# Two solve steps a tick in the second delta-rule unit, other PSUM banks and block order for the output projection, and one product less per norm

## The chip, the cores and the metric

The kernel runs on one NeuronCore of one Trainium2 chip. The metric is the device time of one execution in microseconds; the time of a kernel is the median of its runs. The engines are TensorE (PE, with its weight loads as PEld), VectorE (DVE), ScalarE (ACT), GpSimd (POOL) and SyncE (SP, which issues nearly all DMAs here). Each has its own queue of instructions and works it off in order; they wait for one another by semaphores.

## The reference

One decoder layer over 256 tokens of width 2048, float32. Batch and depth are 1.

```
h = rms_norm(x, ln1)
qkv_a, beta_a, decay_a, z_a, qkv_b, gate_a, gate_b = split(h @ w_in)
y_a = gated_deltanet(qkv_a, beta_a, decay_a, z_a) @ w_branch_a      # 8 heads of 128, chunked delta rule
y_b = moba_attention(rope(q_b), rope(k_b), v_b) @ w_branch_b        # one block of 256: causal attention
x = x + (sigmoid(gate_a) * y_a + sigmoid(gate_b) * y_b) @ w_out
u_gate, u_val = split(causal_dwconv(rms_norm(x, ln2) @ w_up))       # 2 x 5632 channels, width 3
x = x + (silu(u_gate) * u_val) @ w_down
return rms_norm(x, final_norm)
```

The delta rule needs, per head and chunk of tokens, the inverse of a unit lower triangular matrix (`triangular_solve`), and its output is normed per head before it is gated with silu(z_a).

## The kernel before

**Products.** Every weight is split in two parts, high and low (`wh`, `wl`), and so is every activation; three products of parts stand for one float32 product. `load_w` fetches a weight block of 128 x 2048 (SP's queue, four `wraw` buffers), ACT casts it to `wh` in two halves and DVE subtracts to get `wl` (`split`, `low`). There are two `wh`/`wl` buffers, so a block's cast waits until PE has done with the block before the last. `chunk` makes an output of 2 x 128 channels from two blocks, `by_token` (gates, values, z, branches) one of 2 x 128 tokens x 512 channels in two accumulators, from blocks with 4 x 128 input channels each. A gate chunk has 96 products of 512 columns, 24 for each weight block.

**Stages in order.** Input norm and the delta rule's projections, values and z; the attention's projections (`ps_moba`); eight gate chunks (`ps_gate`, the loop at L756); the branch projections (`ps_br`, L800); the output projection (`ps_wo`, L819); 44 chunks of the up-projection (`ps_up`); the down projection (`pd`), the last norm and the output.

**Work in the background.** Heads are worked on in two units of four. `gdn_pair`, `gdn_unit`, `moba` and `merged` are generators in the list `bg`. `main_mm` counts the main products and calls `tick` after each EVERY = 1700 units (8 gate products): every generator in `bg` is advanced by one `yield`. So the generators' instructions are written in between the main products; a scheduler then sets the final order on each engine, within the dependences. `tc.issue_after(lows[-1].ins)` holds an instruction behind the last weight subtraction written so far.

**The unit's path.** `gdn_unit` solves the triangular blocks in 31 steps (L561; two DVE instructions each, on `X` and `tm`), with a `yield` after every second step in unit 0 and after every step in unit 1 (L566). Then X goes to DRAM and comes back as `TL` (POOL's queue, L568 and L570); after 12 ticks DVE transposes it in 32 x 32 blocks (L574). Two levels of products `py` and `pu` follow, then `u0`, `r1`, `u1`, the outputs `po`, POOL's square `so`, the head norm on DVE and ACT (L637 to L645), four ticks, the transposes `pot` and ACT's evictions into `ya`. Unit 1's tail waits for "gates", which is set right ahead of the gate chunks. At c == 4 the loop of L762 advances the generators until unit 1 is at its end; the gates' evictions for that chunk (`gts`, L769) are written behind it. After the eight chunks ACT casts `ya` and `yb` to `yca` and `ycb`, and POOL subtracts for their low parts (L781, L782).

**PSUM.** Up to the branches, pool `ps_mm` has three accumulators of one bank, `ps_sd` five. `psum_pools(3, 2)` then makes three of two banks (`wide`) and two of one. A new accumulator waits until what lay in its banks has been evicted (`reuse_waits="tile"`). For the first output chunk the steps at L821 run both blocks over input channels 0 to 11 and then over 12 to 15 (in units of 128), since `mc`, its input, gets channels 12 to 15 last: they come from `merged(3, i)`, which transposes on PE (`pt_m`) and splits on ACT and DVE (L797, L798).

**Norms.** `rstd` sums squares over channels with products against `ones` in float32 (`R1` at L300 from two tiles, `R2` at L844 from four).

Of the kernel before, what the change touches and what calls it, by code (L numbers as in the profile page):

```python
# [15 lines left out]
ALU = mybir.AluOpType  # L16
AX = mybir.AxisListType
PSUM = bass.MemoryType.PSUM
# [4 lines left out]
KD = D // P  # L23
# [50 lines left out]
def layer_kernel(ctx: ExitStack, tc: tile.TileContext, xT, pos, cst, ceye, vec, convw, ffw, bdv,  # L74
                 w_gdn, w_z, w_bd, w_moba, w_mv, w_gate, w_ba, w_bb, w_o, w_up, w_dn, fnorm, out):
    nc = tc.nc
    pe, act, dve, pool, sp = nc.tensor, nc.scalar, nc.vector, nc.gpsimd, nc.sync
# [8 lines left out]
    def mmg(ps, pairs, start=True, stop=True, **kw):  # L86
        n = len(pairs)
        for i, (a, b) in enumerate(pairs):
            pe.matmul(ps, a, b, start=(start and i == 0), stop=(stop and i == n - 1), **kw)  # L89
# [3 lines left out]
    def tick():  # L93
        for it in list(bg):
            if next(it, bg) is bg:
                bg.remove(it)
# [31 lines left out]
    def load_w(src, n=2048, into=None, piece=1024, raw=None):  # L128
        raw = raw or fetch(src, n)
        wh, wl = into or parts()  # L130
        for o in range(0, n, piece):
            lows.append(split(wh[:, o:o + piece], wl[:, o:o + piece], raw[:, o:o + piece]))
        return wh[:, :n], wl[:, :n]
# [10 lines left out]
    wide = [False]  # L144
    pst = [None, None, None]

    def psum_pools(mm, sd):
        if pst[2]:
            pst[2].close()
        pst[2] = ExitStack()  # L150
        pst[0] = pst[2].enter_context(tc.tile_pool(name="ps_mm", bufs=mm, space=PSUM, reuse_waits="tile"))
        pst[1] = pst[2].enter_context(tc.tile_pool(name="ps_sd", bufs=sd, space=PSUM, reuse_waits="tile"))

    psum_pools(3, 5)

    def mmt(name):
        return pst[0].tile([P, 2, 2, T] if wide[0] else [P, 2, T], F32, name=name, tag="mm")

    def sdt(name):
        return pst[1].tile([P, 512], F32, name=name, tag="sd")  # L160
# [12 lines left out]
    def chunk(blocks, x, kt, name, raws=(None, None), piece=1024, steps=((0, 0, None), (1, 0, None)), flush=None):  # L173
        ps = mmt("ps_" + name)
        ws = {}
        for n, (j, k0, k1) in enumerate(steps):
            while n == flush and bg:
                tick()
            if j not in ws:
                ws[j] = load_w(blocks[j], kt * P, raw=raws[j], piece=piece)  # L180
            block(ps[:, j], ws[j], x, kt, k0, k1)
        return ps
# [32 lines left out]
    def rstd(parts, tp, name):  # L215
        ps = sdt(name)[:, :T]
        mmg(ps, [(ones, t) for t in parts])
        r = tp.tile([P, T], F32, name=name)
        act.activation(r, ps, AF.Sqrt, bias=epst, scale=1.0 / D)
        dve.reciprocal(r, r)  # L220
        return r
# [9 lines left out]
    fk = front.enter_context(tc.tile_pool(name="fk", bufs=1))  # L231
# [51 lines left out]
    sq = []  # L283
# [5 lines left out]
        dve.tensor_tensor(sq[2], sq[2], sq[3], op=ALU.add)  # L289
    dve.tensor_tensor(sq[0], sq[0], sq[2], op=ALU.add)  # L290
    dve.tensor_tensor(sq[0][:, 0:2], sq[0][:, 0:2], sq[0][:, 2:4], op=ALU.add)


    wb2 = g.tile([P, KD, 48], F32R, name="wb2")
# [2 lines left out]
    low(wb2[:, :, 0:16], wb2[:, :, 32:48], wbd)  # L297
    s = sdt("ps_bd")[:48, :T]
    mmg(s, [(wb2[:, k, :], x_[:, k, :]) for k in range(KD) for x_ in (hh, hl)])
    R1 = rstd([sq[0][:, 0, :], sq[0][:, 1, :]], fk, "R1")  # L300
    R1b = both(R1)
    beta = fk.tile([16, T], F32, name="beta")
    sint = fk.tile([48, T], F32, name="sint")
# [81 lines left out]
    def decay():  # L385
        nz, ez, den, sv, s2, pv, spv, gt = (m.tile([16, T], F32, name=n, tag=t) for n, t in (
            ("nz", "qk0"), ("ez", "qk0"), ("den", "qk1"), ("sv", "qk1"), ("s2", "s_"), ("pv", "s_"),
            ("spv", "pT_"), ("gt", "pT_")))
        dve.tensor_tensor(z0, z0, R1[:16, :], op=ALU.mult)
        act.activation(beta, z0, AF.Sigmoid)  # L390
# [33 lines left out]
    def rms_columns():  # L424
        pt = sdt("pt_rms")
        for i in range(2):
            pe.transpose(pt[:, 16 * i:16 * i + 16], R1[:16, i * P:(i + 1) * P], ident[:16, :16])
        dve.tensor_copy(cols[:, 5:].rearrange("p a b -> p (a b)"), pt[:, :32])
# [110 lines left out]
    def gdn_unit(u):  # L539
# [21 lines left out]
        for r in range(30, -1, -1):  # L561
            tm = gu.tile([P, 8, 32], F32, name="tm", tag="Tm", bufs=1)
            n = 32 - r
            dve.tensor_tensor(tm[:, :, :n], X[:, :, r:], N[:, r:r + 1, r:].to_broadcast([P, 8, n]), op=ALU.mult)
            dve.tensor_reduce(X[:, :, r], tm[:, :, :n], axis=AX.X, op=ALU.add, negate=True)
            if r % (2 - u["n"]) == 0:  # L566
                yield
        pool.dma_start(bass.AP(tensor=dT.tensor, offset=dT.offset, ap=[[32 * P + 32, 32], [8 * P, 4], [P, 8], [1, 32]]), X)  # L568
        TL = gu.tile([P, 8, P], F32, name="TL", tag="u", bufs=1)
# [86 lines left out]
    def pair(w, i):  # L656
        return [w[2 * i], w[2 * i + 1]]
# [8 lines left out]
    for n in range(2):  # L666
        u = units[n]
# [3 lines left out]
        for pr in range(2):  # L671
# [3 lines left out]
            for a, t in enumerate((kq[:, 1], kq[:, 0], v)):  # L675
                if gr == 0 and a < 2:
                    ps = (ps_q0, ps_k0)[a]
                else:
                    ps = chunk(pair(w_gdn, 3 * gr + a), hc, KD, "gdn")
# [9 lines left out]
        if n == 0:  # L689
            bg.append(rotary())  # L690

            for c in range(2):
                ps = by_token(w_mv[4 * c:4 * c + 4], hc, KD, "ps_v")
# [49 lines left out]
    for gr in range(4):  # L743
        h0 = 2 * gr
        qk = []
        for a in range(2):
            ps = chunk(pair(w_moba, 2 * gr + a), hc, KD, "moba")
            t = m.tile([P, 2, T], F32, name=f"qk{a}")
# [7 lines left out]
    for c in range(8):  # L756
        ps = by_token(w_gate[4 * c:4 * c + 4], hc, KD, "ps_gate")
# [29 lines left out]
    mc = m.tile([P, KD * 2 * T + 128], F32R, name="mc")[:, SHIFT:SHIFT + KD * 2 * T].rearrange("p (k a t) -> p k a t", a=2, t=T)  # L787
# [12 lines left out]
    for c in range(4):  # L800
        ps = by_token(w_ba[2 * c:2 * c + 2], yc[0], H, "ps_br")
# [3 lines left out]
        ps = by_token(w_bb[2 * c:2 * c + 2], yc[1], H, "ps_br")  # L805
# [11 lines left out]
    sqa = b.tile([P, 2, T], F32, name="sqa", bufs=1)  # L817
    h2 = hp.tile([P, KD, 2, T], F32R, name="h2", tag="hc")
    for c in range(8):  # L819
        if c == 0:  # L820
            steps = ((0, 0, KD - 4), (1, 0, KD - 4), (0, KD - 4, KD), (1, KD - 4, KD))  # L821
            ps = chunk(pair(w_o, c), mc, KD, "wo", steps=steps, flush=2)
            y_st.close()
            bkeep = bk.enter_context(tc.tile_pool(name="bkeep", bufs=1, side="right", reuse_waits="tile"))
            x1 = bkeep.tile([P, KD, T], F32, name="x1")
            ffv = bkeep.tile([P, 88, 4], F32, name="ffv")
            sp.dma_start(ffv, ffw)
        else:
            ps = chunk(pair(w_o, c), mc, KD, "wo")
        if c % 2 == 0:  # L830
            s = slice(2 * c, 2 * c + 4)
            sp.dma_start(x1[:, s, :], xT[:, s, :])
        xc = x1[:, 2 * c:2 * c + 2, :]
        for a in (1, 0):
            dve.tensor_tensor(xc, xc, ps[:, :, a, :], op=ALU.add)
        scaled(xc, ln2v, 2 * c, h2[:, :, 0, :], h2[:, :, 1, :])
        if c == 0:
            act.activation(sqa, xc, AF.Square)
        else:
            sq = b.tile([P, 2, T], F32, name="sq2")  # L840
            act.activation(sq, xc, AF.Square)
            if c < 7:
                pool.tensor_tensor(sqa, sqa, sq, op=ALU.add)
    R2 = rstd([t[:, j, :] for t in (sqa, sq) for j in range(2)], bkeep, "R2")  # L844
    R2b = both(R2)
    bp.close()
    m_st.close()
# [4 lines left out]
    for c in range(NF):  # L852
        ps = chunk([w_up[c], w_up[NF + c]], h2, KD, "up")
        un = b.tile([P, 2, T], F32, name="unf")
        join(un, ps, R2b)
        t = b.tile([P, 2, T], F32, name="cvf")
# [15 lines left out]

    ps_d = ctx.enter_context(tc.tile_pool(name="ps_d", bufs=1, space=PSUM, reuse_waits="tile"))
    pd = [[ps_d.tile([P, 512], F32, name=f"pd{i}_{n}") for n in range(4)] for i in range(2)]
    order = [(1, 2), (1, 3), (0, 2), (0, 3), (1, 0), (1, 1), (0, 0), (0, 1)]

    def residual(i, n):
        for j in range(4):
# [118 lines left out]
```

## Time and profile before

| | us |
|---|---|
| median of 3 runs (1494.28 to 1494.69) | 1494.66 |
| the profiled execution | 1494.29 |
| its span in the profile | 1492.5 |
| PE busy | 1473.2 (99%) |
| DVE busy | 989.9 (66%) |
| ACT busy | 728.8 (49%) |
| POOL busy | 177.2 (12%) |

The profile is one execution on the chip. PE's records overlap, as its products are pipelined: what one takes is read from its start to the next one's start. A wait is put down to the releaser that came last by the profile; where that one had long been done, another was meant. Windows give the granted clock of PE, 1.00 being 2.4 GHz and 0.50 being 1.2 GHz. Tiles are named without their buffer numbers, and a line such as L101 or L108 is that of a helper.

### The profile page before, as it was taken

To read this page: it belongs to the slowest core of one execution; us is meant where nothing else is said; L and a number is where in the kernel's file an instruction comes from. 1 tells how busy PE (TensorE), PEld (TensorE's weight loads), DVE (VectorE), ACT (ScalarE), POOL (GpSimd) and SP (SyncE) were. 2 spreads that over 40 slices of the span, in tenths; PEclk is the share of its full clock that TensorE was granted. 3 is DMA by queue.
4 is the path that set the end of the run, shared out by engine and by line. 5 is a ranking of instruction groups with operands and counts; after the bars stand their busy time and mean duration, and the time that the engine had idled before them with its cause. 6 is when DMAs were issued, how large, how long until landed. Compare 5 with 4: busy or idle time off the path is not lost.

```text
span 1492.5 us, 20716 instructions
## 1 busy us (share of the span) xinstructions
PE 1473.2 (99%) x8383; PEld 1296.7 (87%) x8383; DVE 989.9 (66%) x1397; ACT 728.8 (49%) x969; POOL 177.2 (12%) x135
## 2 busy tenths in 40 slices
PE   9999999999999799999999999999999999999997
PEld 8898899999888688888888888888888888888886
DVE  6997866888844445657766776766767766555554
ACT  5665445554443544435455555555545554444444
POOL 0112000433000400000101111121121110000000
PEclk9999999999999899999999999999999999999999
DMA  9455553544654255556555555555555554555552
GB/s 343 171 189 197 201 184 114 173 159 167 210 194 149 85 210 187 195 210 218 179 218 186 187 192 197 187 184 195 197 175 195 196 187 179 189 190 189 196 196 85
DMA packets 44432, 278.14 MB, mean 186 GB/s; under 512 B 5560, under 2 KB 7664, under 8 KB 12208
## 3 DMA queue, kind: packets, MB, share of 16 engines
q1 hardware_dynamic: 41456, 270.98, 50.7%
q0 software_dynamic: 2016, 3.68, 0.8%
q10 hardware_dynamic: 864, 2.16, 0.4%
q8 instruction: 65, 1.06, 0.3%
q14 instruction: 31, 0.25, 0.0%
HBM read 273.65 MB, written 3.15 MB: 185 GB/s over the span
## 4 chain that ended last, share of the span: by engine, by line
PE 98%; ACT 0%; DMA 0%; DVE 0%; POOL 0%; issue 0%; SPq 0%; DVEq 0%; ACTq 0%; POOLq 0%
PE ps_up L101 33%; PE pd L89 16%; PE ps_gate L101 12%; PE ps_gdn L101 8%; PE ps_moba L101 6%; PE ps_wo L101 6%; PE ps_br L101 6%; PE ps_z L101 3%; PE ps_v L101 3%; PE ps_gdn L257 1%; PE g L89 1%; PE pu L604 0%; PE py L598 0%; DMA xs<-in_xT 0%; PE ps_bd L89 0%; PE po L89 0%
## 5 line engine op out<-in xcount | busy, mean ns | idle before, releaser
L108 DVE TENSOR_TENSOR wl<-wraw,wh 128x1024 fp32r<-128x1024 f32 x496 | 601.3, 1249 | 256.8 <-ACT wh L111 256.6
L111 ACT CAST wh<-wraw 128x1024 fp32r<-128x1024 f32 x496 | 495.3, 1046 | 390.3 <-PE ps_up L101 117.3
L101 PE MATMUL ps_up<-h,wh 128*128 128x512 f32 x1408 | 488.6, 390 | 0.0
L101 PE MATMUL ps_up<-h,wl 128*128 128x256 f32 x1408 | 397.0, 282 | 0.0
L101 PEld LDWEIGHTS ps_up<-h,wh 128*128 128x128 f32 x1408 | 264.2, 188 | 55.4
L101 PEld LDWEIGHTS ps_up<-h,wl 128*128 128x128 f32 x1408 | 266.1, 189 | 0.1
L101 PE MATMUL ps_gate<-wh,hc 128*128 128x512 f32 x512 | 158.4, 395 | 2.8 <-ACT gts L769 2.8
L865 POOL TENSOR_TENSOR acts<-sg,cvf 128x256 f32<-128x256 f32 x44 | 80.8, 1837 | 423.3 <-ACT sg L864 423.3
L89 PE MATMUL pd<-wl,ah 128*128 128x512 f32 x336 | 130.8, 389 | 0.0
L89 PE MATMUL pd<-wh,al 128*128 128x512 f32 x336 | 130.8, 389 | 0.0
L101 PE MATMUL ps_gdn<-hc,wh 128*128 128x256 f32 x704 | 127.1, 281 | 0.0
L101 PEld LDWEIGHTS ps_gate<-wh,hc 128*128 128x128 f32 x512 | 96.7, 190 | 22.9 <-ACT gts L769 3.2
L101 PEld LDWEIGHTS ps_gdn<-hc,wh 128*128 128x128 f32 x704 | 108.3, 188 | 0.4
L859 ACT ACTIVATE cvf<-unf,ffv 128x256 f32<-128x256 f32 x88 | 48.2, 595 | 104.5 <-DVE unf L207 104.5
L101 PE MATMUL ps_gate<-wl,hc 128*128 128x512 f32 x256 | 98.9, 395 | 0.0
L861 DVE SCALAR_TENSOR_TENSOR cvf<-unf,ffv,cvf 128x254 f32<-128x254 f32 (+1 forms) x176 | 77.3, 481 | 32.1 <-ACT cvf L859 31.8
L101 PE MATMUL ps_gdn<-hc,wl 128*128 128x256 f32 x352 | 98.4, 280 | 0.0
L101 PE MATMUL ps_moba<-hc,wh 128*128 128x256 f32 x512 | 92.2, 281 | 0.0
L101 PE MATMUL ps_wo<-mc,wh 128*128 128x512 f32 x256 | 89.0, 390 | 0.4 <-ACT wh L111 0.4
L89 PE MATMUL pd<-wh,ah 128*128 128x512 f32 x336 | 86.7, 391 | 0.0
L111 ACT CAST ah<-acts 128x256 fp32r<-128x256 f32 x44 | 17.9, 406 | 126.0 <-PE pd L89 116.3
L101 PEld LDWEIGHTS ps_moba<-hc,wh 128*128 128x128 f32 x512 | 78.7, 188 | 0.0
(423 smaller groups left out, 1861.6 us busy)
## 6 DMA issues: line engine op xcount, KB each, us to landing
wraw<-in_w_up SPq DMA_DIRECT2D x88, 1024.0 KB, 4.8
wraw<-in_w_dn SPq DMA_DIRECT2D x44, 1024.0 KB, 4.8
wraw<-in_w_gate SPq DMA_DIRECT2D x32, 1024.0 KB, 4.8
wraw<-in_w_gdn SPq DMA_DIRECT2D x22, 1024.0 KB, 4.8
wraw<-in_w_moba SPq DMA_DIRECT2D x16, 1024.0 KB, 4.8
wraw<-in_w_o SPq DMA_DIRECT2D x16, 1024.0 KB, 4.8
wraw<-in_w_z SPq DMA_DIRECT2D x8, 1024.0 KB, 5.4
wraw<-in_w_mv SPq DMA_DIRECT2D x8, 1024.0 KB, 4.8
```

The source lines that it names most:

```text
L89: pe.matmul(ps, a, b, start=(start and i == 0), stop=(stop and i == n - 1), **kw)
L101: pe.matmul(ps, a, b, start=start, stop=stop, skip_group_check=True)
L108: return (eng or dve).tensor_tensor(lo, src, hi.bitcast(F32), op=ALU.subtract)
L111: act.copy(hi, src)
L257: pe.matmul(ps_q0[:, b], r3(wq[b], P)[:, k], xs[:, k], start=(k == b == 0), stop=(k == KD - 1), skip_group_check=True)
L859: act.activation(t[:, j, :], un[:, j, :], AF.Identity, scale=w[:, 2:3], bias=w[:, 3:4])
L861: dve.scalar_tensor_tensor(t[:, j, d:], un[:, j, :T - d], w[:, 2 - d:3 - d], t[:, j, d:], op0=ALU.mult, op1=ALU.add)
L865: pool.tensor_tensor(acts[:, c, :], sg, t[:, 1, :], op=ALU.mult)
```

## The change

```diff
--- before.py
+++ after.py
@@ -148,8 +148,9 @@
         if pst[2]:
             pst[2].close()
         pst[2] = ExitStack()
-        pst[0] = pst[2].enter_context(tc.tile_pool(name="ps_mm", bufs=mm, space=PSUM, reuse_waits="tile"))
-        pst[1] = pst[2].enter_context(tc.tile_pool(name="ps_sd", bufs=sd, space=PSUM, reuse_waits="tile"))
+        for i in ((0, 1), (1, 0))[wide[0]]:
+            pst[i] = pst[2].enter_context(tc.tile_pool(name=("ps_mm", "ps_sd")[i], bufs=(mm, sd)[i], space=PSUM,
+                                                       reuse_waits="tile"))
 
     psum_pools(3, 5)
 
@@ -289,6 +290,7 @@
         dve.tensor_tensor(sq[2], sq[2], sq[3], op=ALU.add)
     dve.tensor_tensor(sq[0], sq[0], sq[2], op=ALU.add)
     dve.tensor_tensor(sq[0][:, 0:2], sq[0][:, 0:2], sq[0][:, 2:4], op=ALU.add)
+    dve.tensor_tensor(sq[0][:, 0], sq[0][:, 0], sq[0][:, 1], op=ALU.add)
 
 
     wb2 = g.tile([P, KD, 48], F32R, name="wb2")
@@ -297,7 +299,7 @@
     low(wb2[:, :, 0:16], wb2[:, :, 32:48], wbd)
     s = sdt("ps_bd")[:48, :T]
     mmg(s, [(wb2[:, k, :], x_[:, k, :]) for k in range(KD) for x_ in (hh, hl)])
-    R1 = rstd([sq[0][:, 0, :], sq[0][:, 1, :]], fk, "R1")
+    R1 = rstd([sq[0][:, 0, :]], fk, "R1")
     R1b = both(R1)
     beta = fk.tile([16, T], F32, name="beta")
     sint = fk.tile([48, T], F32, name="sint")
@@ -563,7 +565,7 @@
             n = 32 - r
             dve.tensor_tensor(tm[:, :, :n], X[:, :, r:], N[:, r:r + 1, r:].to_broadcast([P, 8, n]), op=ALU.mult)
             dve.tensor_reduce(X[:, :, r], tm[:, :, :n], axis=AX.X, op=ALU.add, negate=True)
-            if r % (2 - u["n"]) == 0:
+            if r % 2 == 0:
                 yield
         pool.dma_start(bass.AP(tensor=dT.tensor, offset=dT.offset, ap=[[32 * P + 32, 32], [8 * P, 4], [P, 8], [1, 32]]), X)
         TL = gu.tile([P, 8, P], F32, name="TL", tag="u", bufs=1)
@@ -818,8 +820,8 @@
     h2 = hp.tile([P, KD, 2, T], F32R, name="h2", tag="hc")
     for c in range(8):
         if c == 0:
-            steps = ((0, 0, KD - 4), (1, 0, KD - 4), (0, KD - 4, KD), (1, KD - 4, KD))
-            ps = chunk(pair(w_o, c), mc, KD, "wo", steps=steps, flush=2)
+            steps = ((0, 0, 8), (0, 8, 12), (1, 0, 4), (0, 12, KD), (1, 4, KD))
+            ps = chunk(pair(w_o, c), mc, KD, "wo", steps=steps, flush=1)
             y_st.close()
             bkeep = bk.enter_context(tc.tile_pool(name="bkeep", bufs=1, side="right", reuse_waits="tile"))
             x1 = bkeep.tile([P, KD, T], F32, name="x1")
@@ -841,7 +843,9 @@
             act.activation(sq, xc, AF.Square)
             if c < 7:
                 pool.tensor_tensor(sqa, sqa, sq, op=ALU.add)
-    R2 = rstd([t[:, j, :] for t in (sqa, sq) for j in range(2)], bkeep, "R2")
+            if c == 6:
+                pool.tensor_tensor(sqa[:, 0], sqa[:, 0], sqa[:, 1], op=ALU.add)
+    R2 = rstd([sqa[:, 0, :], sq[:, 0, :], sq[:, 1, :]], bkeep, "R2")
     R2b = both(R2)
     bp.close()
     m_st.close()
@@ -872,7 +876,7 @@
 
     ps_d = ctx.enter_context(tc.tile_pool(name="ps_d", bufs=1, space=PSUM, reuse_waits="tile"))
     pd = [[ps_d.tile([P, 512], F32, name=f"pd{i}_{n}") for n in range(4)] for i in range(2)]
-    order = [(1, 2), (1, 3), (0, 2), (0, 3), (1, 0), (1, 1), (0, 0), (0, 1)]
+    order = [(0, 0), (0, 1), (1, 0), (1, 1), (1, 2), (1, 3), (0, 2), (0, 3)]
 
     def residual(i, n):
         for j in range(4):
```

Unit 1's solve yields after every second step, as unit 0's does. `psum_pools` opens the small accumulators' pool ahead of the large one's when `wide` is set, so the two small ones get banks 0 and 1 and the large ones banks 2 to 7, where they had 6, 7 and 0 to 5. The first output chunk runs its first block over channels 0 to 7, empties `bg`, goes on to 11, then takes the second block's channels 0 to 3, the first block's 12 to 15 and the rest of the second block. The order of the down projection's eight accumulators follows the new banks. Each norm sums one tile more ahead of its products: DVE adds for the first, POOL at c == 6 for the second.

The scheduler's order shows it at three places. On DVE, behind the last step of unit 1's solve (`X`), up to the first masking of `py`; `wl` are weight subtractions, `U<-TL` the transpose. Before:

```order
L565 TENSOR_REDUCE X<-tm 128x8
L108 TENSOR_TENSOR wl<-wraw,wh 128x1024 x16
L574 STREAM_TRANSPOSE U<-TL 128x1024
L108 TENSOR_TENSOR wl<-wraw,wh 128x1024 x2
L599 TENSOR_TENSOR Y<-py,ct 128x16x32
```

After:

```order
L567 TENSOR_REDUCE X<-tm 128x8
L108 TENSOR_TENSOR wl<-wraw,wh 128x1024 x6
L576 STREAM_TRANSPOSE U<-TL 128x1024
L108 TENSOR_TENSOR wl<-wraw,wh 128x1024 x3
L601 TENSOR_TENSOR Y<-py,ct 128x16x32
```

The transpose stands ten subtractions (five weight blocks) further ahead; the solve itself stands where it stood.

On PE, the end of unit 1's path. Before, within the chunk c = 5, behind its 24th product:

```order
L101 MATMUL ps_gate<-wl,hc 128x512
L621 MATMUL u_4652<-vb,U 128x128 x4
L628 MATMUL po<-x,aq 128x128 x4
L89 MATMUL po<-x,aq 128x128 x8
L652 MATMUL pot<-ct,ot 128x128 x8
L101 MATMUL ps_gate<-wh,hc 128x512 x2
```

After, around the last products of the chunk c = 4 (`u1` and `po` stand 65 and 49 to 65 gate products earlier than `pot`):

```order
L101 MATMUL ps_gate<-wl,hc 128x512
L654 MATMUL pot<-ct,ot 128x128
L101 MATMUL ps_gate<-wh,hc 128x512 x2
L654 MATMUL pot<-ct,ot 128x128 x4
L101 MATMUL ps_gate<-wl,hc 128x512
L654 MATMUL pot<-ct,ot 128x128 x3
L101 MATMUL ps_gate<-wh,hc 128x512 x2
```

The products that stood one behind another are spread between gate products, and the last of them stands ahead of the chunk c = 5.

On PE, the start of the output projection, with buffer numbers: `ps_br_5739` is the last branch accumulator (bank 1 in both), `wh_5824` the first block's weights, `pt_m` the last two transposes. Before:

```order
L101 MATMUL ps_br_5739<-wl_5773,ycb_5200 128x512
L794 MATMUL pt_m_5852<-identm_5189,gts_4071 128x128 x4
L101 MATMUL ps_wo_5821<-mc_5213,wh_5824 128x512
L101 MATMUL ps_wo_5821<-mc_5213,wl_5825 128x256
L101 MATMUL ps_wo_5821<-mc_5213,wh_5824 128x512
```

After, behind eight pairs of products of the first block (`ps_wo_5821`, now in banks 2 and 3):

```order
L796 MATMUL pt_m_5846<-identm_5189,gts_4104 128x128 x4
L101 MATMUL ps_wo_5821<-mc_5213,wh_5824 128x512
L101 MATMUL ps_wo_5821<-mc_5213,wl_5825 128x256
L101 MATMUL ps_wo_5821<-mc_5213,wh_5824 128x512
L796 MATMUL pt_m_5853<-identm_5189,gts_4104 128x128 x4
L101 MATMUL ps_wo_5821<-mc_5213,wl_5825 128x256
```

Both transposes now stand inside the first block, and its last four channels run 12 pairs of products before the chunk's end, where they had run 4 pairs before it.

## Rows read from the trace of the kernel before

**Rows 1.** The page's first part: busy us (share of the span) x instructions.
```profile
PE 1473.2 (99%) x8383; PEld 1296.7 (87%) x8383; DVE 989.9 (66%) x1397; ACT 728.8 (49%) x969; POOL 177.2 (12%) x135
```

**Rows 2.** PE's waits over the whole span; columns: us in total, times, longest.
```profile
PE pot L652 <- DVE ot L644: 5.2, 1, 5.2
PE ps_gate L101 <- ACT gts L769: 2.8, 1, 2.8
...
PE ps_wo L101 <- DVE wl L108: 0.7, 1, 0.7
PE ps_wo L101 <- ACT wh L111: 0.4, 1, 0.4
```

**Rows 3.** Timeline of PE around the lump; start us, us, instruction, [idle before <-releaser].
```profile
493.67 1.05 PE L621 MATMUL u<-vb,U 128*128 128x128 f32 x8
494.56 1.06 PE L628 MATMUL po<-x,aq 128*128 128x128 f32 x8
...
502.58 2.39 PE L652 MATMUL pot<-ct,ot 128*128 128x128 f32 x8 [5.18 <-DVE ot L644]
507.74 1.22 PE L101 MATMUL ps_gate<-wh,hc 128*128 128x512 f32 x2 [2.78 <-ACT gts L769]
...
512.66 0.62 PE L101 MATMUL ps_gate<-wh,hc 128*128 128x512 f32 x2
...
517.89 0.62 PE L101 MATMUL ps_gate<-wh,hc 128*128 128x512 f32 x2
```

**Rows 4.** Stretches of 2 us behind the lump: PE busy, granted clock, DMA share, GB/s.
```profile
508.00:510.00 2.00, 2.00 (x5) 0.50 0.00 0
...
512.00:514.00 2.00, 2.00 (x9) 0.95 0.01 4
```

**Rows 5.** Timeline of the other engines around the lump.
```profile
498.16 1.89 POOL L635 TENSOR_TENSOR so<-ot 128x1024 f32<-128x1024 f32 x1 [37.64 <-ACT ot L633]
...
502.08 2.19 DVE L644 SCALAR_TENSOR_TENSOR ot<-ot,st,ya 128x128 f32<-128x128 f32 x8
...
505.00 0.69 ACT L653 ACTIVATE ya<-pot,vc 128x512 f32<-128x512 f32 x1 [0.30 <-PE pot L652]
...
512.63 2.00 ACT L111 CAST wh<-wraw 128x1024 fp32r<-128x1024 f32 x2 [0.22 <-PE ps_gate L101]
```

**Rows 6.** Timeline and DMA issues (KB, us to landing) of the second unit's tile TL.
```profile
405.89 0.90 POOL L570 DMA_DIRECT2D TL<-dT  x1 [2.38 <-DMA dT<-X]
...
TL<-dT POOLq DMA_DIRECT2D x1, 512.0 KB, 6.3
...
444.25 1.24 DVE L574 STREAM_TRANSPOSE U<-TL 128x1024 f32<-128x1024 f32 x1
```

**Rows 7.** Timeline of DVE and ACT at the first blocks of the output projection.
```profile
657.84 0.69 DVE L808 TENSOR_TENSOR gts<-ps_br,gts 128x512 f32<-128x512 f32 x1 [0.18 <-PE ps_br L101]
...
659.88 0.69 DVE L808 TENSOR_TENSOR gts<-ps_br,gts 128x512 f32<-128x512 f32 x1 [0.62 <-PE ps_br L101]
...
661.55 0.58 ACT L797 CAST mc<-pt_m 128x512 fp32r<-128x512 f32 x1
...
663.49 0.68 DVE L798 TENSOR_TENSOR mc<-pt_m,mc 128x512 fp32r<-128x512 f32 x1
...
671.04 3.90 ACT L111 CAST wh<-wraw 128x1024 fp32r<-128x1024 f32 x4 [4.96 <-PE ps_wo L101]
```

**Rows 8.** Timeline of PE at the second norm.
```profile
750.94 1.03 PE L89 MATMUL R<-sqa,ones 128*128 128x256 f32 x4
...
752.04 0.28 PE L101 MATMUL ps_up<-h,wl 128*128 128x256 f32 x1
...
752.39 0.28 PE L101 MATMUL ps_up<-h,wl 128*128 128x256 f32 x1
```

**Rows 9.** Timeline of DVE in windows at its first subtractions behind the lump.
```profile
513.71 1.25 DVE L108 TENSOR_TENSOR wl<-wraw,wh 128x1024 fp32r<-128x1024 f32 x1 [9.30 <-ACT wh L111]
...
514.88 2.32 DVE L108 TENSOR_TENSOR wl<-wraw,wh 128x1024 fp32r<-128x1024 f32 x1
```

## The prediction

> **What bounds the kernel now.** I read the page's busy line first: TensorE (PE) is busy 99% of the span [rows 1], so an edit pays only where it takes products off PE or closes a place where PE stands still. The list of PE's waits comes next: beside the kernel's start it has four entries, 5.2 and 2.8 us inside the gate projection and 0.4 and 0.7 us at the first blocks of the output projection [rows 2]. All four stand at places that the diff touches. The timeline of PE, and then of the other engines at these two places, gives the prices. PE's time there is read from start to start, since the records of neighbours overlap.
>
> **Solve, two steps a tick.** In the kernel before, the fifth gate chunk (c = 4) ends with a loop that runs the second unit's generator to its end. What it issues stands in a lump on PE: u1 starts at 493.67, po at 494.56, pot at 502.58, and the next gate product only at 507.74 [rows 3]. Between po and pot lies a chain through other engines: POOL squares the outputs in 1.89 us from 498.16, VectorE (DVE) reduces, ScalarE (ACT) takes the root, DVE scales from 502.08 [rows 5]; after pot, ACT has two evictions, the second at 505.00, and then the gate evictions, for which PE waits 2.8 us [rows 2, 5]. In the changed kernel the unit needs 16 ticks instead of 31 for the solve. The order on DVE shows it: the 32x32 transpose stands behind 6 subtractions instead of 16, and all the unit's products end before gate product 481, with 65 gate products between u1 and pot. The products themselves remain. So the saving is the lump's length less the price of its products in a dense stream.
>
> Length: 507.74 - 493.67 = 14.07 us. Price: u1's 8 records take 494.56 - 493.67 = 0.89 us; po has 8 and 16 of the same size, 0.89 and 1.78; pot's 8 records are priced like u1's, 0.89 (transposes of the same 128 columns; their own row, 2.39 us, holds waits for DVE, so it is only an upper end). Sum 4.45, saving 9.62 us.
>
> Then the clock. After the stop PE runs at the lower of its two levels, 1.2 GHz: the granted clock is 0.50 from 508 to 510 and 0.95 in 512 to 514 [rows 4]. From 512.66 to 517.89 stand 23 gate products, 0.2274 us each; the 12 from 507.74 to 512.66 took 4.92 instead of 2.73 us [rows 3]. That is 2.19 us more. Gate part: 9.62 + 2.19 = 11.81 us.
>
> What covers the chain now: from the last seven products of po (7/4 x 0.89 = 1.56 us) PE has those and 49 gate products, 11.1 us, together 12.7 us, before pot. In the lump the way from po to pot took 502.58 - 494.56 = 8.02 us, with DVE and ACT otherwise idle. So 4.7 us are left for the weight casts and subtractions that now stand in the same queues; without that cover each us would cost PE one.
>
> The earlier start of the unit's tail needs its data earlier too. The transpose ran at 444.25; ten subtractions less are five weight loads, each 24 products x 0.2274 = 5.46 us, so it comes near 417. Its tile TL was issued on POOL's queue at 405.89 and lands 6.3 us later, at 412.2 [rows 6], since the solve itself keeps its place on DVE. Spare: some 4.8 us. Cost nothing.
>
> New in the sixth chunk (c = 5): ACT runs its two evictions, two gate evictions and eight casts of the branch inputs without the stop that covered them, and the next weight cast queues behind. In the kernel before this took from 505.00 to 512.63, 7.63 us, 0.22 of it idle [rows 5]. Let E be the end of the last product but one of chunk 4. A weight cast pair (2.00 us [rows 5]) starts at E, the first eviction at E + 2.0, the second some 0.7 later, the next weight cast at E + 2.7 + 7.4 = E + 10.1; its first half is done at E + 11.1 and its subtraction, 1.25 us [rows 9], at E + 12.4. PE needs it after 53 gate products (12.05 us) and seven transposes (0.8), near E + 12.7. So 0.3 us to spare if DVE runs freely. POOL, however, subtracts the branch inputs just then. In the kernel before, the first of DVE's four subtractions beside it took 1.25 us and the next 2.32 us [rows 9]. So the wait is between 0 and 0.8 us; I take 0, since the subtraction in question is again the first of its run, and keep 0.8 for the range. Later ones cannot pile up: two at 2.32 us are 4.64 us per load against PE's 5.46.
>
> The Trainium skill (SBUF — State Buffer, Who interferes with whom) says that a VectorE instruction with two SBUF inputs contends with a GpSimd instruction that reads SBUF, and that one of them fully blocks while the other runs. The pair 1.25 and 2.32 us agrees. By that rule taken strictly the first subtraction could be the blocked one, and the sum would be 0.8 us smaller.
>
> **Output projection.** Two edits. The first accumulator pair moves from banks 0 and 1 to banks 2 and 3. Of the last branch accumulators, bank 2 is emptied by the DVE instruction at 657.84, bank 1 by the one at 659.88, which ends at 660.57 [rows 7]; PE's 0.4 us wait ended 0.15 us later. The list names ACT, but the first product waits for two things, and the cast of its own weights was long done, so it is DVE's eviction of bank 1. The new pair waits for bank 2 only, free at 658.5, before PE gets there: 0.4 us saved. The small accumulators of the transposes take banks 0 and 1, and stand behind 8 pairs of products now (8 x 0.35 = 2.8 us; a pair is 752.39 - 752.04 = 0.35 [rows 8]), after bank 1 is free: no new wait.
> The 0.7 us is a subtraction that came late, because its cast at 671.04 waited until the first block's weights had been used up [rows 7]. With the new steps the first block ends 12 pairs before the chunk does instead of 4, so that cast starts 8 pairs, 2.8 us, earlier against a wait of 0.7: all of it goes. What could be late next is the last transpose's way into mc (0.58 us on ACT, 0.68 on DVE [rows 7]); behind it PE has about 2.5 + 4 pairs, 2.3 us: covered. Saved: 1.1 us; that it comes back as another wait is a rival below.
>
> **One product less per norm.** Two products take two passes each, so four records. From R's start at 750.94 to the first small product of the next stream is 752.04 - 750.94 = 1.10 us, of which the 512-column product before it has two thirds of a pair, 0.23; 0.87 for two, 0.43 for one. Over the two norms 0.86 us; by the records' own 1.03 us it would be 1.0 [rows 8]. The added sums lie on DVE before the first norm, where PE has a 32-product block to run, and on POOL at c = 6, a whole chunk before its reader: nothing.
>
> **Order of the down projection.** It follows the banks that come free, now 0, 1, 4 to 7 and 2, 3 instead of 6, 7, 2 to 5 and 0, 1. The list of waits has no entry there, and the last up-projection's banks stay last. Zero.
>
> **Sum.** 11.81 + 1.1 + 0.86 = 13.8 us. The profiled execution took 1494.29 us (span 1492.5 and 1.8 around it), which gives 1480.5; the median of the runs is 0.37 higher, so 1480.9 us. The bounds: 0.8 less for the subtraction at c = 5 and 1.5 less if pot's transposes cost their own row's 2.39 us in a dense stream too, 0.2 more by the dearer R. That is 11.5 to 14.0 saved, 1480.7 to 1483.2.
>
> **Rivals.**
> - The queue of c = 5 bites: ACT's eight casts come later than worked out, or POOL blocks the first subtraction. PE waits 0.8 to 2.5 us: 1481.7 to 1483.4. For it: 0.3 us of cover. Against: the waits do not repeat. 16%.
> - The output projection keeps its 1.1 us in another wait (a bank, the transposes): 1482.0. 8%.
> - The norm chain outlasts its cover of 4.7 us: DVE or POOL is held up, PE stops before pot again, and with a stop as long as before the clock drops for another 2.19 us. Some 3 to 5 us and 2.2: 1484 to 1488. 4%. The same would show if the tail were not out of the way before product 481; the order on PE speaks against that.
> - Slower than before: the transpose reaches DVE's head before TL has landed. Behind it on DVE are the weight subtractions, for which PE waits us for us. TL would have to come over 4.8 us later than its 6.3 us before PE notices, and 4.8 + 13.8 = 18.6 us later for the kernel to be slower, say 25 us: 1501. Against: nothing else moves on that queue. 2%.
>
> **How the numbers follow.** 70% for the forecast, 30% for the four rivals. The range 1479.8 to 1483.6 takes in the bounds, the first two rivals and a little below for prices that were set high. A measurement here tells 0.2% (3 us) from no change; only the last rival and part of the third end there, so faster 0.97, same 0.015, slower 0.015.
>
> **What would show it.** Right: the list of PE's waits without pot, gate and output-projection entries; granted clock 1.00 through the gate stage; the transpose near 417 us; two records of R less in each norm. Wrong: a PE wait on a DVE subtraction in the sixth gate chunk (first rival), on ot (third), or DVE idle before the transpose on TL (last).

## The result and the profile after

The changed kernel took 1480.99 us, the median of 4 runs (1480.40 to 1481.47), beside 1494.47 for the kernel before in the same comparison. The ratio is 0.991, with a 95% interval from 0.9893 to 0.9927, so the gain of 0.9% is clear of the noise. The forecast was 1480.9 us, with a range from 1479.8 to 1483.6. The profiled execution took 1480.40 us with a span of 1478.6, 13.9 less than before.

The page's first part of the changed kernel answers to [rows 1], and its list of PE's waits to [rows 2] (columns as there):

```profile
PE 1467.6 (99%) x8379; PEld 1293.3 (87%) x8379; DVE 991.6 (67%) x1398; ACT 728.2 (49%) x969; POOL 178.5 (12%) x136
```

```profile
PE ps_gdn L258 <- DMA xs<-in_xT: 1.7, 1, 1.7
...
```

All four entries of [rows 2] are gone, and nothing has taken their place; the only other entry is the 1.0 us of the first instruction, as before. The wait for xs at the start was 0.9 us in the kernel before; the change doesn't touch it, and its length differs from profile to profile. PE has four records less, two per norm.

**Where the time went** is read best from the first record of each stage's product. The view by tile gives for each group count, duration min/median/max in ns, and first and last start. Before:

```profile
L101 PE MATMUL ps_gate<-wh,hc x512: 387/389/796, 365.7 to 569.3; 128*128 128x512 f32 x171
...
L101 PE MATMUL ps_br<-wh,yca x128: 389/389/477, 569.8 to 648.3; 128*128 128x512 f32 x128
...
L101 PE MATMUL ps_wo<-mc,wh x256: 390/390/467, 660.7 to 750.6; 128*128 128x512 f32 x128
...
L101 PE MATMUL ps_up<-h,wh x1408: 390/390/580, 751.6 to 1240.5; 128*128 128x512 f32 x176
```

After:

```profile
L101 PE MATMUL ps_gate<-wh,hc x512: 387/389/481, 365.6 to 557.5; 128*128 128x512 f32 x171
...
L101 PE MATMUL ps_br<-wh,yca x128: 389/389/478, 557.9 to 636.5; 128*128 128x512 f32 x128
...
L101 PE MATMUL ps_wo<-mc,wh x256: 390/390/484, 647.8 to 737.1; 128*128 128x512 f32 x128
...
L101 PE MATMUL ps_up<-h,wh x1408: 390/390/580, 737.7 to 1226.5; 128*128 128x512 f32 x176
```

A stage lasts from its first start to the next one's. The same subtraction in every profile gives this table (us; the starts are rounded to 0.1, so a length can be off by 0.1; the last column is when the gate stage begins):

| kernel | gates | branches | output projection and norm | up-projection | gates begin |
|---|---|---|---|---|---|
| before | 204.1 | 90.9 | 90.9 | 489.2 | 365.7 |
| after | 192.3 | 89.9 | 89.9 | 489.2 | 365.6 |
| solve_alone | 192.3 | 91.0 | 90.8 | 489.2 | 365.8 |
| steps_alone | 204.4 | 90.9 | 90.1 | 489.2 | 366.0 |
| banks_alone | 204.4 | 89.8 | 91.3 | 489.2 | 365.5 |
| norms_alone | 204.3 | 90.9 | 90.5 | 489.2 | 365.4 |
| filled_stop | 202.6 | 90.9 | 90.9 | 489.1 | 367.7 |
| dose16 | 199.8 | 89.8 | 89.9 | 489.2 | 365.7 |
| dose20 | 203.5 | 89.8 | 89.9 | 489.2 | 365.7 |
| sq2 | 194.1 | 89.8 | 89.9 | 489.2 | 365.7 |
| ticks3 | 192.1 | 89.9 | 89.9 | 489.2 | 368.9 |
| extra_casts | 193.5 | 89.9 | 89.9 | 489.2 | 365.8 |
| r2_one | 192.3 | 89.8 | 89.7 | 488.5 | 367.2 |
| best | 192.2 | 89.9 | 89.6 | 488.6 | 367.9 |

A stage that an edit doesn't touch keeps its length within 0.3 us in all fourteen profiles (the 0.3 in gate stages in which the granted clock falls, 0.1 elsewhere), so terms of half a microsecond can be read here which the medians can't tell. Before to after: gates -11.8, branches -1.0, output projection with norm -1.0, all ahead of the gates -0.1, together 13.9. From the first to the last start of its products the down projection takes 243.2 and 243.1 us.

At the place of the lump, the timeline of PE in the changed kernel (start us, us, instruction) has no gap:

```profile
490.69 0.40 PE L101 MATMUL ps_gate<-wl,hc 128*128 128x512 f32 x1
490.92 0.27 PE L654 MATMUL pot<-ct,ot 128*128 128x128 f32 x1
490.95 0.71 PE L101 MATMUL ps_gate<-wh,hc 128*128 128x512 f32 x2
491.50 0.60 PE L654 MATMUL pot<-ct,ot 128*128 128x128 f32 x4
491.86 0.48 PE L101 MATMUL ps_gate<-wl,hc 128*128 128x512 f32 x1
492.18 0.49 PE L654 MATMUL pot<-ct,ot 128*128 128x128 f32 x3
492.43 0.70 PE L101 MATMUL ps_gate<-wh,hc 128*128 128x512 f32 x2
492.97 0.39 PE L101 MATMUL ps_gate<-wl,hc 128*128 128x512 f32 x1
```

From 490.69 to 492.97 stand six gate products (1.36 us at 0.2274 each) and the eight records of pot, which therefore cost 0.92 us: the 0.89 of the prediction, not the 2.39 of [rows 3].

### The profile page after: what moved, and what is told of

The parts are those of the page before. It is cut to its first block, busy times and chain, and to the rows that moved or that the text cites. A ratio compares the mean times of both kernels' runs of the same rounds, so it can differ in the third digit from the quotient of the medians.

```text
span 1478.6 us, 20705 instructions
## 1 busy us (share of the span) xinstructions
PE 1467.6 (99%) x8379; PEld 1293.3 (87%) x8379; DVE 991.6 (67%) x1398; ACT 728.2 (49%) x969; POOL 178.5 (12%) x136
## 4 chain that ended last, share of the span: by engine, by line
PE 99%; DMA 0%; SPq 0%; DVE 0%; ACT 0%; issue 0%; DVEq 0%; ACTq 0%
PE ps_up L101 33%; PE pd L89 16%; PE ps_gate L101 12%; PE ps_gdn L101 8%; PE ps_moba L101 6%; PE ps_wo L101 6%; PE ps_br L101 6%; PE ps_z L101 3%; PE ps_v L101 3%; PE ps_gdn L258 1%; PE g L89 1%; PE pu L606 0%; PE py L600 0%; DMA xs<-in_xT 0%; PE ps_bd L89 0%; PE po L89 0%
## 5 line engine op out<-in xcount | busy, mean ns | idle before, releaser
L101 PE MATMUL ps_up<-h,wh 128*128 128x512 f32 x1408 | 488.6, 390 | 0.0
L89 PE MATMUL pd<-wh,ah 128*128 128x512 f32 x336 | 92.8, 391 | 0.0
```

The costliest lines, as they stand in the source:

```text
L101: pe.matmul(ps, a, b, start=start, stop=stop, skip_group_check=True)
```

## The experiments

**The solve alone.** `if r % 2 == 0:` put into the kernel before, nothing else.

> The kernel before with the solve's edit alone. My sum: 11.8 us less (9.6 from the lump of the unit's products, 2.2 from the clock behind it), about 1482.7 us; in PE's waits pot and gate are gone, the output projection's 0.4 and 0.7 stand as before; granted clock 1.00 from 484 to 515. Rival, the wait moves on into the next gate chunk (weight subtraction held up by the eight casts or by POOL): an entry of 0.5 us or more for PE behind a DVE subtraction there, and 0.5 to 2.5 us less gain, 1483.2 to 1485.2.

Measured: 1482.9 us (1482.61 to 1483.63, 5 runs) beside 1494.48, ratio 0.9923 (0.9911 to 0.9936). The gate stage falls from 204.1 to 192.3 us as in the full change, and the granted clock is 1.00 in every stretch from 496 to 516. PE's list keeps the output projection's 0.7 and 0.4. The whole gate term, clock included, belongs to this one edit.

**The stop filled.** The kernel before, in `gdn_unit` for the second unit:

```diff
+        if u["n"]:
+            fl = sdt("fill")
+            with tc.issue_after(last.ins):
+                for _ in range(20):
+                    pe.matmul(fl[:, :P], ones, ones, start=True, stop=True)
...
+            with tc.issue_after(last.ins):
+                for _ in range(14):
+                    pe.matmul(fl[:, :P], ones, ones, start=True, stop=True)
```

In the first part `last` is the last product into `po`, in the second the last transpose `pot`; the lines that set it are left out here.

> The kernel before, with products that nobody reads put on PE in the two waits of the lump: 20 of 128 columns behind the last po, 14 behind the last pot, some 4.4 and 3.1 us, each a little shorter than the wait it lies in. The stop keeps its length of 14.1 us. If the slow products behind the stop come from the clock, and the clock from PE standing still, the granted clock stays near 1.00 in 508 to 512, the 12 gate products take 2.7 instead of 4.9 us, and the kernel gets 2.2 us faster, about 1492.3 us. Rival: they are slow for another reason (operands that come late, ACT's crowded queue): 4.9 us as before and 1494.5 us.

Measured: 1492.99 us (11 runs), ratio 0.9989 (0.998 to 0.9998), so 1.5 us less instead of 2.2 (1.5 by the gate stages too, 204.1 to 202.6). The stretch that had 0.50 in [rows 4], in this kernel:

```profile
508.00:510.00 2.00, 2.00 (x18) 1.92 (x17) 0.00 (x0) 1.99 (x4) 0.00 (x0) 1.00 0.00 0
```

(PE, PEld, DVE, ACT and POOL busy, granted clock, DMA share, GB/s.) PE's timeline behind the stop:

```profile
509.45 0.71 PE L101 MATMUL ps_gate<-wh,hc 128*128 128x512 f32 x2
...
512.31 0.62 PE L101 MATMUL ps_gate<-wh,hc 128*128 128x512 f32 x2
...
515.03 1.19 PE L101 MATMUL ps_gate<-wh,hc 128*128 128x512 f32 x4
516.64 0.50 PE L101 MATMUL ps_gate<-wl,hc 128*128 128x512 f32 x1 [0.43 <-DVE wl L108]
516.98 0.62 PE L101 MATMUL ps_gate<-wh,hc 128*128 128x512 f32 x2
```

The clock stayed at 2.4 GHz although the stop lasted as long (13.9 us from u1 to the next gate product), and the 12 products took 512.31 - 509.45 = 2.86 us instead of 4.92: 2.06 gained. So the slow products came from PE standing still, and the term of 2.19 us is right to 0.1. The Trainium skill (TensorE: Matmul & The Clock Gate, What's actually happening) says that the gate goes by how busy PE has been lately; products that nobody reads served as well as real ones here, which agrees. The missing part is the new wait at 516.64: four products of 0.91 us and then 0.7 us more, and 0.1 behind it. In the kernel before the low clock had hidden that the sixth chunk's weight subtraction comes late. Faster PE meets it.

**Output projection, in two halves.** First the new steps with the earlier emptying of `bg` (`flush=1`) alone:

> The kernel before with the new steps of the first output chunk and the earlier emptying of the background list, the banks as before. My sum: the 0.7 us behind a weight subtraction goes, the 0.4 us at the first product stays: 1493.8 us. Rival: the transposes' way into mc or a bank is late instead and PE waits 0.5 us or more there: 1494.5 us.

then the order of the PSUM pools (and of the down projection) alone:

> The kernel before with the small accumulators' banks ahead of the large ones (and the down projection's order that goes with it). My sum: PE's first product of the output projection waits for bank 2 only, the 0.4 us goes and the 0.7 us stays: 1494.1 us. Rival, the list of waits is right that it was the weight cast on ACT: 0.4 us stays, 1494.5 us. The down projection's order: nothing either way.

Measured: 1493.6 us (ratio 0.9994, 0.9985 to 1.0003) and 1493.68 (0.9995, 0.9986 to 1.0004), both beside 1494.48. The times alone can't tell either from no change; the lists can. With the steps the 0.7 is gone and the 0.4 stands. With the banks the 0.4 is gone and the 0.7 stands, so the 0.4 was DVE's eviction of the bank, not the cast that the list names. By the stage table the steps give 0.8 us (90.9 to 90.1) and the banks 0.7 (branches 1.1 less, output projection 0.4 more, since the two groups of `pt_m` move from the one to the other): 1.5 together where I had 1.1. The rows of the kernel before say why:

```profile
659.45 0.39 PE L101 MATMUL ps_br<-wl,ycb 128*128 128x512 f32 x1
659.68 0.60 PE L794 MATMUL pt_m<-identm,gts 128*128 128x128 f32 x4
660.72 0.47 PE L101 MATMUL ps_wo<-mc,wh 128*128 128x512 f32 x1 [0.44 <-ACT wh L111]
...
672.35 0.39 PE L101 MATMUL ps_wo<-mc,wh 128*128 128x512 f32 x1
673.40 0.39 PE L101 MATMUL ps_wo<-mc,wl 128*128 128x256 f32 x1 [0.67 <-DVE wl L108]
```

and the joint in the changed kernel:

```profile
647.56 0.40 PE L101 MATMUL ps_br<-wl,ycb 128*128 128x512 f32 x1
647.79 0.39 PE L101 MATMUL ps_wo<-mc,wh 128*128 128x512 f32 x1
...
650.57 0.60 PE L796 MATMUL pt_m<-identm,gts 128*128 128x128 f32 x4
650.93 0.48 PE L101 MATMUL ps_wo<-mc,wh 128*128 128x512 f32 x1
```

From start to start the first joint took 660.72 - 659.45 = 1.27 us. One product (0.23) and one `pt_m` group (650.93 - 650.57 = 0.36) account for 0.59; 0.68 was lost, not 0.44. The second took 1.05 us, of which 0.23 is the product: 0.82 lost, not 0.67. The list counts idle time between records, and a record runs on past the next one's start.

**One product less per norm, alone.**

> The kernel before with one product less in each norm and the two added sums, nothing else. My sum: two records of R less per norm, 0.43 us each, 0.9 us in all, 1493.6 us. Rival: a product waits for the added sum (PE entry behind DVE sq in the first norm or POOL sqa in the second, 0.4 us or more): no change, 1494.5 us.

Measured: 1493.76 us beside 1494.75, ratio 0.9994 (0.9986 to 1.0003), 1.0 less by the medians, which the times alone can't tell from no change; no entry for the added sums in PE's list, and the stage of the second norm is 0.4 us shorter. From R's first start to the first product with `wl` behind it, 36.55 to 37.64 us in the kernel before became in the changed one

```profile
36.84 0.59 PE L89 MATMUL R<-sq,ones 128*128 128x256 f32 x2
...
37.51 0.28 PE L101 MATMUL ps_gdn<-hc,wl 128*128 128x256 f32 x1
```

1.09 to 0.67, so 0.42 us; the second norm's 1.10 [rows 8] became 0.66 (737.44 to 738.10), so 0.44. Together 0.86, as the prediction had it.

**How much of the solve's edit is needed.** More ticks in the second unit: `if r % 2 == 0 or u["n"] and r < 16:`, and the same with 20.

> The changed kernel with 24 ticks for the second unit's solve in place of 16 (the last 16 steps yield one by one). In the order on PE 23 gate products stand between the last po and pot, and pot stands ahead of the 25th product of the sixth chunk, as in the kernel before. If the norm chain takes what it took in the lump (5.4 us from the last po to pot), 23 products cover it but for 0.1 us; then PE waits some 2.8 us for the gate evictions behind pot: about 1484 us, 1486 if the clock falls for so short a stop. If it takes what it took in the changed kernel, where weight subtractions share DVE (9.1 us from the last po to the end of ot), PE waits 3.9 us ahead of pot, then 2.8, and the clock falls: 1488 to 1490.

> The same with 26 ticks: 4 gate products between the last po and pot, 0.9 us. By the lump's chain PE waits 4.4 us ahead of pot and 2.8 behind it, and the clock falls as in the kernel before (2.2 us): some 9.4 us over the changed kernel, 1490.4. By the longer chain 8.2 and 2.8 us and the clock: 1494 us. If nothing but the stop counts, and not where it lies, this and the run with 24 ticks differ by the difference of their waits ahead of pot.

Measured: 1487.82 us (ratio 0.9951, 0.9938 to 0.9965) and 1491.28 (0.9975, 0.9966 to 0.9984). PE's waits with 24 ticks and with 26:

```profile
PE ps_gate L101 <- ACT gts L771: 2.8, 1, 2.8
...
PE pot L654 <- DVE ot L646: 0.7, 2, 0.4
```

```profile
PE pot L654 <- DVE ot L646: 4.2, 1, 4.2
PE ps_gate L101 <- ACT gts L771: 2.8, 1, 2.8
```

Ahead of pot the short chain holds: 23 products cover it nearly, 4 leave 4.2 us (expected 4.4). My times, 1486 with the clock lost and 1490.4, were low by 1 to 2 us for two reasons. Behind pot I had counted the listed 2.8 alone, but pot's records themselves follow `ot` one by one: with 26 ticks it took 506.83 - 501.66 = 5.2 us from pot to the next gate product, of which 0.9 is pot's price. And the clock, lost in both, cost more with 24 ticks than the 2 us that I had put. Behind the stop, the timeline of PE with 24 ticks reads

```profile
502.69 1.22 PE L101 MATMUL ps_gate<-wh,hc 128*128 128x512 f32 x2 [2.78 <-ACT gts L771]
...
508.75 0.40 PE L101 MATMUL ps_gate<-wl,hc 128*128 128x512 f32 x1
```

and the granted clock is 0.50 from 502 to 508: 14 products in 6.06 us instead of 3.18. The cost over the changed kernel adds up to its 7.5 us of gate stage: 0.6 ahead of pot, 4.0 from pot to the gates, 2.9 by the clock. The shorter stop lost more by the clock than the long one of the kernel before (2.2), so between these two this part of the price didn't go down with the length of the stop.

**The norm chain made longer.** In the changed kernel `pool.tensor_tensor(so, ot, ot, op=ALU.mult)` is written three times for the second unit.

> The changed kernel with POOL's square of the second unit's outputs written three times instead of once, so that the norm chain is 3.8 us longer; the result is the same. By the prediction's step the chain had 4.7 us of cover left: no wait ahead of pot and 1481 us. By the trace of the changed kernel ot was done only 2.1 us ahead of pot, and the eight casts behind pot leave the next weight subtraction no time to spare: then pot and all behind it on ACT come some 2 to 3 us later, PE waits that long at the next weight block, behind a DVE subtraction or the gate evictions, and the time is 1483 to 1484.5 us, with 2 us more if the clock falls.

Measured: 1482.23 us (ratio 0.9915, 0.99 to 0.993); the gate stage is 1.8 us longer than in the changed kernel. The three squares took 7.56 us, since DVE's subtractions ran beside them, and `ot` came 5.6 us later. PE's waits:

```profile
PE ps_gate L101 <- ACT gts L772: 0.6, 1, 0.6
...
PE ps_gate L101 <- DVE wl L108: 0.4, 1, 0.4
```

None of it stands ahead of pot: the scheduler had put pot 15 gate products further back. The delay came out behind pot, in the evictions and the weight cast that ACT does next. The clock stayed at 1.00 there. The chain grew by more than the 3.8 us that I had set, so this run doesn't decide how much cover there was; it shows where the price of this delay is paid, and that it is less than the delay.

**The queue of c = 5 loaded.** The changed kernel with `if nm_ == "b" and i < 2: act.copy(yp.tile([P, 2, T], F32, name="spare"), t[:, s])` behind the casts.

> The changed kernel with two more casts of 512 columns among the eight of c = 5, 0.52 us each on ACT; nobody reads what they write. If the next weight cast has no time to spare there (the trace of the changed kernel: PE's weight load waited 0.2 us for the subtraction), PE waits 1.0 to 1.1 us behind a DVE subtraction and the time is 1482.0 us. By the prediction's 0.3 us of cover it would be 0.7 us and 1481.7. If the queue catches up before PE needs it: no entry and 1481.0.

Measured: 1482.3 us (ratio 0.9914, 0.99 to 0.9929), gate stage 1.2 us longer. PE's timeline:

```profile
503.35 0.39 PE L101 MATMUL ps_gate<-wl,hc 128*128 128x512 f32 x1
503.84 1.21 PE L101 MATMUL ps_gate<-wh,hc 128*128 128x512 f32 x4
505.69 0.50 PE L101 MATMUL ps_gate<-wl,hc 128*128 128x512 f32 x1 [0.64 <-DVE wl L108]
```

Lost: 0.49 - 0.23 = 0.26 ahead of the casts' half block and 1.85 - 0.91 = 0.94 ahead of the subtraction's, 1.2 us for 1.04 us of casts. So that queue had no time to spare.

**Further than the change.** `if r % (2 + 1 * u["n"]) == 0:`, three steps a tick in the second unit.

> The changed kernel with three solve steps a tick in the second unit (11 ticks in place of 16). In the order the transpose stands behind 4 weight subtractions instead of 6 and pot at gate products 429 to 432, in the middle of a chunk. DVE reaches the transpose near 410.5 us and TL lands at 412, so DVE should wait 1 to 2 us on TL there, the last rival's mechanism in small. My theory: PE does not notice (it has 4.8 us), the c = 5 queue loses two evictions and a table load, and PE's weight load no longer waits 0.2 us there: 1480.9 us, the same within 0.2. Last rival: PE waits for the subtraction behind the transpose, 1 to 2 us, 1482 to 1483 us.

Measured: 1479.81 us (1479.48 to 1483.44, 4 runs), ratio 0.9903 (0.9888 to 0.9918). DVE waits for TL, and PE does not notice: the three entries of PE's list all belong to the start.

```profile
415.38 1.25 DVE L576 STREAM_TRANSPOSE U<-TL 128x1024 f32<-128x1024 f32 x1 [1.58 <-DMA TL<-dT]
```

The last rival's mechanism, DVE held up by TL, is real, and 1.6 us of it don't reach PE; how much more would, no run shows. By the two decimals of the timelines the gate stage is some 0.15 us shorter than in the changed kernel (561.02 - 368.87 against 557.92 - 365.61): with pot out of the way no gate product of c = 5 waits, each starts 0.23 us after the one before.

**One more product, and the start.** First the changed kernel with one product in the second norm (`dve.tensor_tensor` adds the last squares' halves and `sqa[:, 0]`, `rstd([sq[:, 0, :]], ...)`):

> The changed kernel with the second norm down to one product: DVE adds the two halves of the last squares and the running sum ahead of it (two instructions of 256 columns). By the price of a product 2 x 0.43 = 0.87 us less, 1480.1 us, with two R records in place of six. Rival: DVE's sums come late and PE or the first eviction of the up-projection waits: no gain, 1481.0.

then that with three steps a tick and `act.dma_start(xs[:, h, :], ...)`:

> Three solve steps a tick, the second norm with one product, and the eight transfers of the input xs issued by ACT instead of SP, beside the weights' transfers. At the start PE waited 1.7 us for xs in the trace of the changed kernel, since SP issues the sixteen transfers one by one, 0.43 us each. If the issue is what holds xs back, that wait falls by 1 to 1.7 us, and with the norm's 0.9 us the time is 1478.4 to 1479.1 us. Rival: the transfers share the same 16 engines and the later weights come late instead (an entry behind wraw or xs of the same size): 1480.1 us.

Measured: 1479.48 us (ratio 0.9897, 0.9882 to 0.9912) and 1481.31 (0.9907, 0.989 to 0.9923). The single product gains 0.9 us by the stages (output projection 0.2 and up-projection 0.7 less), as expected. Issuing xs from ACT lost more than it gave; PE's list:

```profile
PE ps_gdn L258 <- DVE wraw L255: 1.8, 3, 1.4
PE ps_gdn L101 <- DVE wl L108: 1.3, 1, 1.3
```

The wait for xs is gone and the weights come late in its place, the rival, but the loss is 1.2 us larger than it had said. Part of it can lie in ACT's own queue: ACT issues the transfers ahead of its scaling of xs, which began at 11.08 us instead of 5.50 in r2_one; its first weight cast came at 21.27 instead of 19.33, and behind that cast stands the 1.3 us wait. How the loss divides between the transfers and ACT's queue isn't shown. So r2_one and ticks3 are the fastest kernels run, 1.2 to 1.5 us below the changed one by medians of different comparisons, of which the stages show 0.9 and 0.15; for the rest they show no place. The two edits without the third were not run together.

## Why the prediction was right, point by point

- **Gate stage, 11.81 us.** Measured 11.8 by the stages (11.9 with what the next point takes back), and the solve's edit alone gives it. Both of its parts hold: the lump's length (pot costs 0.92 us in a dense stream) and the clock (2.06 us come back when the same stop is filled).
- **The queue of c = 5, priced at 0, with 0 to 0.8 as bounds.** It costs some 0.1 us: 0.06 at the product of 504.33 below, and at most the 0.15 by which the stage is shorter with three steps a tick. The rows of DVE, POOL and PE in the changed kernel:

```profile
502.62 1.61 DVE L108 TENSOR_TENSOR wl<-wraw,wh 128x1024 fp32r<-128x1024 f32 x1 [7.43 <-ACT wh L111]
...
504.16 2.32 DVE L108 TENSOR_TENSOR wl<-wraw,wh 128x1024 fp32r<-128x1024 f32 x1
```

```profile
501.85 1.31 POOL L108 TENSOR_TENSOR ycb<-yb,ycb 128x512 fp32r<-128x512 f32 x1
...
503.10 2.29 POOL L108 TENSOR_TENSOR ycb<-yb,ycb 128x512 fp32r<-128x512 f32 x1
```

```profile
503.42 1.07 PE L101 MATMUL ps_gate<-wh,hc 128*128 128x512 f32 x4
504.33 0.46 PE L101 MATMUL ps_gate<-wl,hc 128*128 128x512 f32 x1
504.62 0.62 PE L101 MATMUL ps_gate<-wh,hc 128*128 128x512 f32 x2
```

  I took 1.25 us for the first subtraction, the first of its run in [rows 9]. It took 1.61: POOL's instruction had begun 0.77 us earlier and ended at 503.16, and DVE finished 1.07 us after that. Each then waits for the other (2.29 and 2.32 us). The Trainium skill (SBUF — State Buffer, Who interferes with whom) says that one blocks fully while the other runs; these rows agree. The price was 0.36 us, less than the 0.54 that POOL's instruction still had to run. The cover of 0.3 us is eaten: the subtraction ends at 504.23, its product starts at 504.33 and the next 0.29 us later instead of 0.23. That it cost almost nothing is a near miss, and luck: in extra_casts 1.04 us of delay there cost 1.2. The rival with 16% had its mechanism right and lacked only a little.
- **Cover of the norm chain, 4.7 us left.** It was 4.0. The rows of PE and DVE in the changed kernel:

```profile
478.22 1.72 PE L89 MATMUL po<-x,aq 128*128 128x128 f32 x14
```

```profile
481.76 3.05 DVE L108 TENSOR_TENSOR wl<-wraw,wh 128x1024 fp32r<-128x1024 f32 x2 [6.69 <-ACT wh L111]
...
486.65 2.19 DVE L646 SCALAR_TENSOR_TENSOR ot<-ot,st,ya 128x128 f32<-128x128 f32 x8
```

  From the start of po's last products (478.22) to the end of the first piece of `ot` (486.65 and an eighth of 2.19) the changed kernel took 8.7 us, since two weight subtractions, 3.05 us beside POOL's square, stand ahead of the reduction on DVE; pot began at 490.92. The 8.0 of the prediction ran from po's first product (494.56); from the same last 14 products, which began at 495.67, the way to pot was 6.9 us in the kernel before. So the chain grew by 1.8 us, of which the cover shows only 0.7, as the 8.0 was 1.1 too long. I had said that this work must fit into the cover without taking it off. In the expectation for sq2 I went wrong the other way: 2.1 us is from the end of the last piece to the first pot, but pot follows `ot` piece by piece.
- **Output projection, 1.1 us.** The term that was mis-sized: 1.5 by the two single edits, 1.6 by the two stages (2.0 less the second norm's 0.44). The mechanism was right at both places. The prices came from the list of waits, against the prediction's own rule to read PE from start to start; by that rule they are 0.68 and 0.82, the 0.1 that remains lying in the product after the wait.
- **Norms, 0.86 us.** Measured 0.42 and 0.44. The added sums cost nothing.
- **Zero terms.** Down projection 243.2 and 243.1. The transpose ran at 415.90 (said: near 417) with no wait; TL, issued at 405.74, landed 6.1 us later, so 4.1 us were to spare instead of 4.8. With three steps a tick DVE waited 1.6 us for TL and PE none.
- **The sum.** 11.8 + 1.6 + 0.86 = 14.3; the profile's span fell by 13.9. The start of that execution was 0.3 us later than before (R at 36.84 instead of 36.55), which took back most of what I had given too little for the output projection. By the medians, 1494.47 to 1480.99, it was 13.5 where the prediction had 13.8, from a median of 1494.66. So the forecast's closeness to 0.1 us is partly luck; the terms are good to half a microsecond.

## What to carry to other kernels

Where one engine is busy all the time, difference the first records of its stages in two profiles: the table told terms of 0.4 us that no median of 11 runs could. Price a wait from start to start of the records around it, and if the engine stood still long enough for its clock to fall, add the slow products behind it, which here did not shrink with the stop. When a stop is taken away, look at once at the queue behind it: here the work that the stop had covered had then no time to spare, and in sq2 a longer chain showed up there rather than where it grew.

## What the runs showed of the hardware

- **The spread of the profiles lies at the start.** The first norm's R starts between 36.3 and 40.1 us and the gate stage between 365.4 and 368.9 us in the fourteen profiles, while untouched stages behind agree. PE's wait for the first transfers of xs goes from 0.5 to 2.6 us in the thirteen that issue them from SP; in the three profiles with 2.0 us or more (filled_stop, r2_one, ticks3) the granted clock falls there too, in the others not. The profiled execution of ticks3 was 3.4 to 4.0 us slower than its other runs, and its stretch from 10 to 15 us reads

```profile
10.00:15.00 5.00, 5.00 (x13) 3.99 (x12) 4.99 (x10) 4.93 (x10) 0.00 (x0) 0.51 1.05 388
```

  so there the late transfer was paid once as a wait and again at 1.2 GHz.
- **A short stop is enough for the lower clock, but not every one.** A wait of 2.8 us with 0.7 ahead of it (dose16) lowered it for 14 products; one of 0.6 us (sq2) and the 1.7 us at the start of the changed kernel did not.
- **A second issuing queue did not start PE sooner.** With xs issued by ACT, PE's first product waited for the weights' scaling instead, which DVE began at 6.30 us against 4.84 in r2_one, and started at 7.05, against 5.58 there.
